# Six MLP batches begin with a product whose PSUM bank ScalarE first copies two columns of the last output into

## The chip, the core and the metric

The kernel runs on one core of one Trainium2 chip. The metric is the device time of one launch in microseconds (us); three runs of the kernel before took 1219.04, 1220.44 and 1220.67 us, median **1220.44 us**. The core's engines work beside each other and wait for each other by semaphores: TensorE multiplies (PE in the profile; the loads of its weights are listed apart, as PEld), ScalarE (ACT) casts, copies and evaluates functions, VectorE (DVE) adds and subtracts, GpSimd (POOL) does little here, and SyncE (SP) issues the transfers from the chip's memory. TensorE writes its products into eight banks of a memory called PSUM, from which ScalarE and VectorE read.

## The reference

Two residual layers with a mixer and an MLP each; the change is in the MLP, which is the last line of the loop:

```python
def reference(x, c, ada_w, ada_b, norm_mix, norm_mlp, ..., mlp_w1, mlp_w2):
    for layer in range(DEPTH):
        mod = c_act @ ada_w[layer] + ada_b[layer]
        shift1, scale1, gate1, shift2, scale2, gate2 = jnp.split(mod[:, None, :], 6, axis=-1)
        ...
        h = rms_norm(x, norm_mlp[layer]) * (1.0 + scale2) + shift2
        x = x + gate2 * (jnp.square(jax.nn.relu(h @ mlp_w1[layer])) @ mlp_w2[layer])
    return x
```

x is 512 tokens by 1024, the hidden layer has 4096 columns, and all is in 32-bit floating point.

## The kernel before

**Precision.** Every operand of a product is split in two, hi (the number rounded to the type in which TensorE multiplies) and lo (what is left). `mm3` makes one product out of three matmuls: weights hi by data hi (L290), weights hi by data lo (L291), weights lo by data hi (L292). These three lines carry nearly all that TensorE does. A weight block comes by a transfer (`raw_w`, L269, the profile's `wraw`), is cast on ScalarE to `whi` (L280) and subtracted on VectorE to `wlo` (L281); `split_w` does both, in rings of four buffers each, and `at` says at which column of its buffer the block begins: `AT512` at 0, `AT256` at 16.

**The MLP** (`mlp`, called once for each layer: about 298 to 600 us and 913 to 1220 us) goes in four batches of 1024 hidden columns. In a batch

- first come four *pairs* (`pair`; in the first batch of a layer fewer, since part of its hidden columns is made before). A pair makes 256 hidden columns of all 512 tokens by a scheme of seven products of half size. A product is 4 x 3 matmuls of 128x256. Its operands are parts of the weights (`wa`, `wb`, `wc`, `wd`) and of the data (`hT`, and sums `t1` to `t4`, the profile's `t0h` to `t3l`), where `wb` and `wc` are split from sums and differences of two weight blocks that VectorE forms in buffers called `tt` (L1081 to L1087), and `wd` (`wdh`, `wdl`) is half of a block. The banks are `a`, `b`, `c`, 256 columns each. `a` gets the first, the third, the sixth and the seventh product, and the content of `a` after the first and after the third is copied out by ScalarE (`kept`, L1114), after the first one so that the third can go on adding in the bank;
- the seventh product of a pair (`wd` by `t4`) is put off (`last`, `before()`, `rest()`) until after the second product of the next pair, or, behind the last pair of a batch, until after the first output's seventh step;
- then come the outputs: 8 (7 or 5 in a layer's last batch) sums of 128x512, each 8 x 3 matmuls with 512 columns, over the hidden columns just made. `products` runs them, `done` adds them to x on VectorE (`x_add`, L515) and asks for the weights and the bank of the output after the next (`second`).

`acc` gives out the eight banks in turn.

**What sets the order.** On TensorE the order is written out by hand: matmuls run in the order of the code. On ScalarE, VectorE and SyncE a scheduler places the instructions, which then run in that order on each engine. `tc.issue_after(i)` makes instructions begun within it stand behind `i`.

**The start of a batch.** Behind the first batch of a layer each batch is prepared while the outputs of the one before run: ahead of the products of output n-2 `pair_w` (a generator with three steps) is started and taken two steps, to `wa` and `wb`; behind that output's addition it is taken the third, to `wc` and `wd`. After the products of output n-1, and `done`, the next batch's first pair starts. There are six such starts: batches 1, 2 and 3 of both layers.

Of the kernel before, what the change touches and what calls it, by code (L numbers as in the profile page):

```python
# [220 lines left out]
def trunk(tc, x_d, c_d, rep_d, small_d, const_d, ada_d, ws_d, win_d, wv_d, woab_d, w1_d, w2_d, wqk_d, wvc_d, woc_d, out_d):  # L221
    nc = tc.nc
    act, dve, pool_e, pe, sync = nc.scalar, nc.vector, nc.gpsimd, nc.tensor, nc.sync
# [137 lines left out]
    def acc():  # L361
        return mps.tile([P, T], F32, name="acc", tag="acc", bufs=4)
# [374 lines left out]
    for j in range(2):  # L737
        copied = act.copy(Q2[:, j], sacc[6 + j])
# [250 lines left out]
    w = [load_w(woab_d[o]) for o in (0, 1, 2)]  # L989
# [78 lines left out]
    def pair_w(l, i, hp):  # L1068


        r0, r1 = raw_w(w1_d[l, 2 * i]), raw_w(w1_d[l, 2 * i + 1])
        a, b = slice(0, T), slice(T, 2 * T)

        def place():
            nsum[0] += 1
            n = (nsum[0] - 1) % 4
            return tt[:, 1024 * n:1024 * n + 1024]
        w = [split_w(r0, None, AT256)]
        yield w
        s_ = place()  # L1080
        dve.tensor_tensor(s_[:, a], r1[:, a], r1[:, b], op=ALU.add)  # L1081
        dve.tensor_tensor(s_[:, b], s_[:, a], r0[:, a], op=ALU.subtract)
        w.append(split_w(s_, None, AT256))
        yield w
        z_ = place()
        dve.tensor_tensor(z_[:, a], r0[:, b], s_[:, b], op=ALU.subtract)
        dve.tensor_tensor(z_[:, b], r0[:, a], r1[:, a], op=ALU.subtract)  # L1087
        w.append(split_w(z_, None, AT256))
        w.append([hp.tile([P, 576], F32R, name=n, tag=n)[:, 16:528] for n in ("wdh", "wdl")])
        split(r1[:, b], *w[3])  # L1090
        yield w

    def pair(i, hp, th, hid, before, steps_):


        for w in steps_:
            pass
        wa, wb, wc, wd = w
        a, b, c = [acc(256) for _ in range(3)]
        cm = [hp.tile([P, T], F32, name="cm", tag="cm", bufs=3) for _ in range(2)]  # L1100
        out = [hid_new(hp, 2 * i + j) for j in range(2)]
        hid += out
        b11 = [(hT[k], H[0]) for k in range(4)]
        b21 = [(hT[k], H[0]) for k in range(4, 8)]
        b22 = [(hT[k], H[1]) for k in range(4, 8)]
        t1, t2, t3, t4 = [[(t_, slice(256 * k, 256 * k + 256)) for k in range(4)] for t_ in th]

        def prod(ps, w, at, bs, first):
            for k, (h, sl) in enumerate(bs):
                mm3(ps, w, slice(at + k * P, at + (k + 1) * P), h, sl, first and k == 0, k == 3, skip_group_check=True)  # L1110

        def kept(ps):
            t_ = hp.tile([P, 256], F32, name="kept", tag="kept", bufs=5)
            act.copy(t_, ps)  # L1114
            return t_

        def relu2(j, sl, ps=None):
            c_ = cm[j][:, sl]
            act.activation(c_, c_ if ps is None else ps, AF.Relu)
            act.activation(c_, c_, AF.Square)  # L1120
            split(cm[j], *out[j], sl)

        prod(a, wa, 0, b11, True)
        p1 = kept(a)
        prod(c, wb, 0, t1, True)
        p5 = kept(c)
        before()
        prod(a, wb, T, t2, False)
        u2 = kept(a)
        prod(b, wa, T, b21, True)  # L1130
        dve.tensor_tensor(cm[0][:, H[0]], b, p1, op=ALU.add)
        prod(c, wc, 0, b22, False)
        dve.tensor_tensor(cm[0][:, H[1]], c, u2, op=ALU.add)
        relu2(0, FULL)
        prod(a, wc, T, t3, False)
        dve.tensor_tensor(cm[1][:, H[1]], a, p5, op=ALU.add)
        relu2(1, H[1])

        def last():
            prod(a, wd, 0, t4, False)  # L1140
            relu2(1, H[0], a)
        return last
# [15 lines left out]
    def mlp(l, last, hp, head, th, more=()):  # L1158

        nrm = Norm(1, 0, (7,)) if not last else None  # L1160
        ahead = None
        for b in range(4):
            hid, rest = list(head) if b == 0 else [], lambda: None
            if b == 0:
                for n, j in enumerate((4, 5)):
                    whole_tile(more[n] if more else load_w(w1_d[l, j]), j, hp, hid)
            for i in range(len(hid) // 2, 4):
                rest = pair(4 * b + i, hp, th, hid, rest, ahead or pair_w(l, 4 * b + i, hp))
                ahead = None
            n = 8 if b < 3 else 7 if last else 5  # L1170
            second = lambda o: (acc(), load_w(w2_d[l, b // 2, o, b % 2], None, AT256 if o == n - 1 else AT512))

            def products(p, k0, k1):
                for k in range(k0, k1):
                    mm3(p[0], p[1], ks(k), hid[k], FULL, k == 0, k == 7)

            def done(o):
                added = x_add(o, ps_[o][0], FULL, l, GATE2)
                if b == 3:
                    if last:  # L1180
                        sync.dma_start(out_d[o], x[o])
                    else:
                        nrm.add(o, FULL)
                if o + 2 < n:
                    ps_[o + 2] = second(o + 2)
                if o < len(PIECES[b]):

                    with tc.issue_after(added.ins):
                        background(PIECES[b][o])

            ps_ = {0: second(0)}
            products(ps_[0], 0, 7)
            rest()
            ps_[1] = second(1)
            products(ps_[1], 0, 7)
            for o in range(2):
                products(ps_[o], 7, 8)
                done(o)
            for o in range(2, n):
                if o == n - 2 and b < 3:  # L1200

                    ahead = pair_w(l, 4 * b + 4, hp)
                    next(ahead)
                    next(ahead)
                products(ps_[o], 0, 8)
                done(o)
                if o == n - 2 and b < 3:
                    ahead = [next(ahead)]
        if not last:
            log_exp_tables()  # L1210
        ps, banks, ws = {}, {}, []
        for o in range(n, 8):
            for hf in range(2):
                banks[bank[0] % 8] = o, hf
                ps[o, hf] = acc(256)

            ws.append(load_w(w2_d[l, 1, o, 1], None if o == n else (hp, f"t{o - 6}h", f"t{o - 6}l"), AT256))
        return nrm, ps, banks, hid, ws
# [44 lines left out]
    hp = pool("mlp0", stack=m_s)  # L1263
# [396 lines left out]
    hid = [tuple(Handle(t=t_) for t_ in hl) for hl in hk_t]  # L1660
# [11 lines left out]
    w = [weights(wqk_d[s // 2, s % 2], None, AT256) for s in range(4)]  # L1672
# [21 lines left out]
    for s_ in "v0 q2 q3 u0 u1 v1 w0 q4 v2 q5 u2 q6 u3 q7 v3 u4 u6 w1 u5 u7".split():  # L1694
        n = int(s_[1])
# [32 lines left out]
    th = [[in_h1([P, 1088], F32R, f"t{i}{a}").new(AT512) for a in "hl"] for i in range(4)]  # L1728
# [109 lines left out]
```

## Time and profile before

| | us |
|---|---|
| median of three runs | 1220.44 |
| the execution that was profiled | 1222.3 |
| its span, first to last instruction | 1220.5 |
| TensorE busy, MLP of layer 0 (298 to 600) | 301.33 of 302 |
| VectorE busy there | 212.34 |
| ScalarE busy there | 150.88 |
| TensorE busy, MLP of layer 1 (913 to 1220) | 303.98 of 307 |
| VectorE busy there | 178.08 |
| ScalarE busy there | 140.43 |

The mean clock granted to TensorE is 0.997 of full speed over the span and 1.00 in both MLP stages. The share of time in which the transfer engines are busy is 0.44 in the first stage and 0.30 in the second.

How to read it: matmuls are pipelined, each begins while the one before is still running, so a TensorE that is busy without a gap may still run its matmuls closer together or farther apart. What a stretch of matmuls costs is the distance from the start of one to the start of the next, and that is read from a stretch without a pause as its length over its number of matmuls. A row of the timeline has start, duration, engine, line, operation, output and inputs, and in brackets the idle time of the engine ahead of it with what ended it. In the rows of one line (L1114 ...) three durations stand after the count: the shortest, the middle and the longest, in ns, and then the times of the first and the last. A row of the waits has who waited, for whom, us in all, how often, and the longest.

### The profile page before, as it was taken

What the parts mean: (1) busy time and instruction counts of PE and PEld (TensorE: products, weight loads), DVE (VectorE), ACT (ScalarE), POOL (GpSimd) and SP (SyncE); (2) the same over time, 40 slices, a digit from 0 to 9 for tenths busy, and PEclk for the clock granted to TensorE, in tenths of its full rate; (3) what the DMA queues carried; (4) which work ended last, traced back from release to release, by engine and by line L of the source; (5) the groups of instructions that cost most, each with busy time, mean ns of one, the idle gap of its engine ahead of it and who ended that gap; (6) DMA issues with size and microseconds to landing.
All of it is one profiled execution on the core that took longest, in us unless ns stands there. A gap on an engine that the chain in (4) does not pass through costs nothing.

```text
span 1220.5 us, 19156 instructions
## 1 busy us (share of the span) xinstructions
PE 1205.6 (99%) x7657; PEld 1067.4 (87%) x7657; DVE 890.1 (73%) x1433; ACT 610.6 (50%) x1101; POOL 15.3 (1%) x25
## 2 busy tenths in 40 slices
PE   8999999999999999999999999999999999999998
PEld 6788877899889899898998888888998898998997
DVE  8997878769577675866768885888796575566652
ACT  4343233438247255274547764677574282472650
POOL 0000000000000000000220000000000000000000
PEclk9999999999999999999989999999999999999999
DMA  8765453612533523624435424534114233233131
GB/s 300 259 233 164 144 202 125 204 52 69 200 101 133 193 83 121 207 87 158 153 93 184 139 86 156 173 121 136 39 56 137 68 122 120 70 122 104 62 130 52
DMA packets 46330, 163.50 MB, mean 134 GB/s; under 512 B 5264, under 2 KB 5784, under 8 KB 46240
## 3 DMA queue, kind: packets, MB, share of 16 engines
q1 hardware_dynamic: 46240, 162.27, 39.9%
q8 instruction: 60, 0.98, 0.3%
q14 instruction: 30, 0.25, 0.1%
HBM read 155.96 MB, written 2.10 MB: 130 GB/s over the span
## 4 chain that ended last, share of the span: by engine, by line
PE 84%; DVE 9%; DMA 4%; ACT 2%; issue 1%; SPq 0%; ACTq 0%; DVEq 0%
PE b L290 20%; PE b L292 20%; PE b L291 20%; PE acc L290 4%; PE acc L292 3%; PE acc L291 3%; PE b L1590 1%; PE b L1569 1%; PE b L1625 1%; DMA raw<-in_ws 1%; PE b L1626 1%; PE b L1627 1%; PE b L1497 1%; DVE eraw L429 1%; DVE wlo L281 1%
## 5 line engine op out<-in xcount | busy, mean ns | idle before, releaser
L280 ACT CAST whi<-wraw 128x1024 fp32r<-128x1024 f32 x123 | 127.1, 1047 | 199.8 <-PE b L291 86.4
L290 PE MATMUL b<-hidh,whi 128*128 128x512 f32 (+1 forms) x544 | 205.5, 378 | 0.0
L291 PE MATMUL b<-hidl,whi 128*128 128x512 f32 (+1 forms) x544 | 205.3, 377 | 0.0
L292 PE MATMUL b<-hidh,wlo 128*128 128x512 f32 (+1 forms) x544 | 205.1, 377 | 0.0
L290 PE MATMUL b<-hh,whi 128*128 128x256 f32 (+1 forms) x632 | 195.7, 310 | 0.0
L291 PE MATMUL b<-hl,whi 128*128 128x256 f32 (+1 forms) x632 | 192.6, 305 | 0.6 <-DVE hl L1453 0.5
L292 PE MATMUL b<-hh,wlo 128*128 128x256 f32 (+1 forms) x632 | 192.4, 304 | 0.0
L281 DVE TENSOR_TENSOR wlo<-wraw,whi 128x1024 fp32r<-128x1024 f32 x123 | 149.4, 1221 | 44.1 <-ACT whi L280 41.5
L515 DVE SCALAR_TENSOR_TENSOR x<-b,modc,x 128x512 f32<-128x512 f32 (+1 forms) x100 | 67.8, 683 | 87.2 <-PE b L292 87.0
L291 PEld LDWEIGHTS b<-hl,whi 128*128 128x128 f32 x632 | 121.2, 192 | 5.5 <-DVE hl L1453 0.9
L290 PEld LDWEIGHTS b<-hh,whi 128*128 128x128 f32 x632 | 119.9, 190 | 5.7 <-issue 1.4
L292 PEld LDWEIGHTS b<-hh,wlo 128*128 128x128 f32 x632 | 120.0, 190 | 5.3
L292 PEld LDWEIGHTS b<-hidh,wlo 128*128 128x128 f32 x544 | 102.2, 188 | 19.3
L291 PEld LDWEIGHTS b<-hidl,whi 128*128 128x128 f32 x544 | 102.4, 188 | 18.5
L290 PEld LDWEIGHTS b<-hidh,whi 128*128 128x128 f32 x544 | 102.1, 188 | 18.7
L281 DVE TENSOR_TENSOR wlo<-tt,whi 128x1024 fp32r<-128x1024 f32 x52 | 63.5, 1220 | 30.4 <-ACT whi L280 29.5
L280 ACT CAST whi<-tt 128x1024 fp32r<-128x1024 f32 x52 | 53.3, 1048 | 61.4 <-PE b L291 50.1
L429 DVE CUSTOM_DVE_ANT_0 wraw<-wraw,cb 128x1024 f32<-128x1024 f32 x56 | 67.9, 1219 | 13.5 <-DMA wraw<-in_ada 13.4
L300 DVE TENSOR_TENSOR hidl<-cm,hidh 128x256 fp32r<-128x256 f32 (+1 forms) x90 | 44.8, 510 | 39.2 <-ACT hidh L299 37.4
L290 PE MATMUL acc<-hh,whi 128*128 128x512 f32 x128 | 52.2, 408 | 0.0
L1391 DVE TENSOR_TENSOR wlo<-raw,whi 128x1024 fp32r<-128x1024 f32 x36 | 43.8, 1220 | 9.9 <-ACT whi L1390 9.8
L292 PE MATMUL acc<-hh,wlo 128*128 128x512 f32 x128 | 49.9, 390 | 0.0
(377 smaller groups left out, 2664.2 us busy)
## 6 DMA issues: line engine op xcount, KB each, us to landing
wraw<-in_w SPq DMA_DIRECT2D x122, 512.0 KB, 3.6
wraw<-in_ada SPq DMA_DIRECT2D x56, 512.0 KB, 3.5
raw<-in_ada SPq DMA_DIRECT2D x24, 512.0 KB, 4.2
eraw<-in_ada SPq DMA_DIRECT2D x16, 512.0 KB, 3.7
wraw<-in_win SPq DMA_DIRECT2D x16, 512.0 KB, 3.4
raw<-in_wqk SPq DMA_DIRECT2D x16, 512.0 KB, 4.5
raw<-in_ws SPq DMA_DIRECT2D x8, 512.0 KB, 6.4
wraw<-in_woab SPq DMA_DIRECT2D x8, 512.0 KB, 3.9
```

Of the source, the lines that this page charges most:

```text
L280: act.copy(hi, raw)
L281: dve.tensor_tensor(lo, raw, hi.bitcast(F32), op=ALU.subtract)
L290: pe.matmul(ps, whi, h[0][:, hs], start=start, stop=False, **kw)
L291: pe.matmul(ps, whi, h[1][:, hs], start=False, stop=False, **kw)
L292: pe.matmul(ps, wlo, h[0][:, hs], start=False, stop=stop, **kw)
L300: dve.tensor_tensor(lo[:, sl], t_[:, sl], hi[:, sl].bitcast(F32), op=ALU.subtract)
L429: dve.tensor_tensor_reduce(out=raw, in0=raw, in1=cbt[0], scale=1.0, scalar=0.0, op0=ALU.mult, op1=ALU.add, accum_out=modr[:, col:col + 1])
L515: return dve.scalar_tensor_tensor(x[o][:, sl], ps, mcol(l, v, o), x[o][:, sl], op0=ALU.mult, op1=ALU.add)
L1391: on_dve(1024, lambda: dve.tensor_tensor(lo.t, raw.t, hi.t.bitcast(F32), op=ALU.subtract), (raw, hi), (lo,), 1)
L1497: pe.matmul(col.t[:, 8 * s + 2 * b:8 * s + 2 * b + 2], sq[s].t[:, ks(b)], hs2, start=True, stop=True)
L1569: pe.transpose(tp.t[:, o_:o_ + P], be.t[:, w0:w0 + P], ident)
L1590: pe.matmul(po.t[orow, P * b - t0:P * (b + 1) - t0], v.t[:, c, hcol], be.t[:, w0:w0 + P], start=first[j], stop=(c == b), skip_group_check= ...
```

## The change

Before the addition of the last output (n-1) of a batch, `mlp` takes the next bank with `acc(256)` and has ScalarE copy two columns of the last output's bank into it. This bank is then handed to the next batch's first pair, which uses it as its `a`; so no bank is used that would not have been used, and the first product overwrites what was copied. The third step of `pair_w` no longer runs behind output n-2: it runs in `pair`, within `tc.issue_after` of the copy, so the instructions that it issues on ScalarE stand behind the copy. So do those of the second pair of the batch, since `copied` is cleared only there.

```diff
-    def pair(i, hp, th, hid, before, steps_):
-
-
-        for w in steps_:
-            pass
+    copied = [None]
+
+    def pair(i, hp, th, hid, before, steps_, first=None):
+
+
+        with ExitStack() as after:
+            if copied[0] is not None:
+
+                after.enter_context(tc.issue_after(copied[0]))
+            for w in steps_:
+                pass
         wa, wb, wc, wd = w
-        a, b, c = [acc(256) for _ in range(3)]
+        if first is None:
+            copied[0] = None
+        a, b, c = [acc(256) if n or first is None else first for n in range(3)]
...
-        ahead = None
+        ahead = bank_ = None
...
-                rest = pair(4 * b + i, hp, th, hid, rest, ahead or pair_w(l, 4 * b + i, hp))
-                ahead = None
+                rest = pair(4 * b + i, hp, th, hid, rest, ahead or pair_w(l, 4 * b + i, hp), bank_)
+                ahead = bank_ = None
...
                 products(ps_[o], 0, 8)
+                if o == n - 1 and b < 3:
+
+
+                    bank_ = acc(256)
+                    copied[0] = act.copy(bank_[:, 0:2], ps_[o][0][:, 0:2]).ins
                 done(o)
-                if o == n - 2 and b < 3:
-                    ahead = [next(ahead)]
```

The order of instructions on TensorE, SyncE and GpSimd is the same as before. It moves on ScalarE and VectorE. The line numbers below are those of each kernel's own file: what is L1114 before is L1122 after the change, and what is L1131 is L1139.

ScalarE at the start of the first of the six batches, before. `x4` means four such rows in a run; `b_3140` is the bank `a` of the batch's first product.

```order
L280 CAST whi<-wraw 128x1024 x4
L299 CAST wdh<-wraw 128x512
L280 CAST whi<-wraw 128x1024
L280 CAST whi<-tt 128x1024 x2
L280 CAST whi<-wraw 128x1024
L1114 COPY kept<-b_3140 128x256
L1114 COPY kept<-b_3142 128x256
L280 CAST whi<-tt 128x1024
L1114 COPY kept<-b_3140 128x256
```

The same place after. `b_3059` is the bank of the last output, `b_3129` the bank of the first product.

```order
L280 CAST whi<-wraw 128x1024 x5
L280 CAST whi<-tt 128x1024
L1218 COPY b_3129<-b_3059 128x2
L280 CAST whi<-tt 128x1024
L299 CAST wdh<-wraw 128x512
L280 CAST whi<-wraw 128x1024
L1122 COPY kept<-b_3129 128x256
L1122 COPY kept<-b_3143 128x256
L280 CAST whi<-tt 128x1024
L1122 COPY kept<-b_3129 128x256
```

The copy has come in, and the casts of the third weights (the second `whi<-tt`) and of `wdh` now stand behind it, together with the cast for the next pair's first weights and ahead of the first `kept`.

VectorE at the same place, before; `x_66` to `x_68` are the additions of the last three outputs to x (`b_3059` again the last output's bank), `cm<-b_...,kept` the additions of a pair.

```order
L515 SCALAR_TENSOR_TENSOR x_66<-b_2995,modc,x_66 128x512
L281 TENSOR_TENSOR wlo<-tt,whi 128x1024
L1082 TENSOR_TENSOR tt<-tt,wraw 128x512
L1086 TENSOR_TENSOR tt<-wraw,tt 128x512
L1081 TENSOR_TENSOR tt<-wraw 128x512
L1082 TENSOR_TENSOR tt<-tt,wraw 128x512
L515 SCALAR_TENSOR_TENSOR x_67<-b_3027,modc,x_67 128x512
L281 TENSOR_TENSOR wlo<-tt,whi 128x1024
L1086 TENSOR_TENSOR tt<-wraw,tt 128x512
L1087 TENSOR_TENSOR tt<-wraw 128x512
L515 SCALAR_TENSOR_TENSOR x_68<-b_3059,modc,x_68 128x512
L281 TENSOR_TENSOR wlo<-wraw,whi 128x1024
```

The same place after.

```order
L515 SCALAR_TENSOR_TENSOR x_66<-b_2995,modc,x_66 128x512
L281 TENSOR_TENSOR wlo<-tt,whi 128x1024
L1086 TENSOR_TENSOR tt<-wraw,tt 128x512
L515 SCALAR_TENSOR_TENSOR x_67<-b_3027,modc,x_67 128x512
L515 SCALAR_TENSOR_TENSOR x_68<-b_3059,modc,x_68 128x512
L281 TENSOR_TENSOR wlo<-tt,whi 128x1024
L300 TENSOR_TENSOR wdl<-wraw,wdh 128x512
L281 TENSOR_TENSOR wlo<-wraw,whi 128x1024
L281 TENSOR_TENSOR wlo<-tt,whi 128x1024
L1139 TENSOR_TENSOR cm<-b_3142,kept 128x256
L281 TENSOR_TENSOR wlo<-tt,whi 128x1024
L1141 TENSOR_TENSOR cm<-b_3143,kept 128x256
```

The third weights' subtraction and that of `wdl` now stand behind the last addition to x, which the copy precedes; the operations on `tt` that prepare a later pair no longer stand between the last additions but later in the batch.

## The prediction, made before the changed kernel was run

> **What bounds the kernel now.** I read the page first: engine shares, granted clock, chain.
>
> ```profile
> PE 1205.6 (99%) x7657; PEld 1067.4 (87%) x7657; DVE 890.1 (73%) x1433; ACT 610.6 (50%) x1101; POOL 15.3 (1%) x25
> PEclk9999999999999999999989999999999999999999
> PE 84%; DVE 9%; DMA 4%; ACT 2%; issue 1%; SPq 0%; ACTq 0%; DVEq 0%
> ```
>
> TensorE is busy nearly always, at the full clock, and carries 84% of the chain. ScalarE has half its time free. The change touches only the two MLP stages, so next I asked who TensorE waits for there (298 to 600 us, then 913 to 1220 us); each answer has one row.
>
> ```profile
> PE b L292 <- DVE wlo L281: 0.7, 1, 0.7
> PE b L292 <- DVE wlo L281: 0.3, 1, 0.3
> ```
>
> One microsecond in 609. Both waits stand in a first batch; at the six batch starts that the change edits, TensorE waits for nothing. So no wait is there to remove, and a gain can only come from matmuls that follow each other faster. Busy time does not show that, since matmuls are pipelined, so I divided stretches without a pause by the matmuls that start in them. The table by windows has stretch, length, busy time (count), clock, DMA share and GB/s; its count includes one to three matmuls still running from before.
>
> ```profile
> 352.93:391.09 38.16, 38.16 (x325) 1.00 0.30 99
> 1133.61:1171.77 38.16, 38.16 (x326) 1.00 0.30 99
> 282.26:287.70 5.44, 5.44 (x50) 1.00 0.01 3
> 302.35:307.79 5.44, 5.44 (x51) 1.00 0.39 133
> 916.41:921.85 5.44, 5.44 (x51) 1.00 0.36 112
> 312.57:313.98 1.41, 1.41 (x13) 1.00 0.00 0
> 604.88:607.83 2.95, 2.95 (x27) 1.00 0.00 0
> ```
>
> The first two rows are the pair products of the first and the last of the six batches: 27 products of 12 matmuls, 128x256 each (the 28th runs later, between two outputs). 38.16 us over 324 matmuls is 117.8 ns each. The next three rows hold 48 matmuls of the same shape, same offset of weights to operand and same clock: 5.44/48 = 113.3 ns. **So TensorE has two spacings for this product, 4% apart, and each holds as long as nothing interrupts.** What precedes the short ones is seen in the timeline.
>
> ```profile
> 299.81 1.23 DVE L281 TENSOR_TENSOR wlo<-tt,whi 128x1024 fp32r<-128x1024 f32 x1 [0.39 <-ACT whi L280]
> 300.02 0.28 PE L290 MATMUL b<-t0h,whi 128*128 128x256 f32 x1
> 300.14 0.28 PE L291 MATMUL b<-t0l,whi 128*128 128x256 f32 x1
> 301.09 0.19 PEld L292 LDWEIGHTS b<-t0h,wlo 128*128 128x128 f32 x1 [0.87 <-DVE wlo L281]
> 301.09 0.38 PE L292 MATMUL b<-t0h,wlo 128*128 128x256 f32 x1 [0.67 <-DVE wlo L281]
> 301.31 0.28 PE L290 MATMUL b<-t0h,whi 128*128 128x256 f32 x1
> 301.43 0.29 PE L291 MATMUL b<-t0l,whi 128*128 128x256 f32 x1
> 301.67 0.28 PE L290 MATMUL b<-t0h,whi 128*128 128x256 f32 x1
> 301.78 0.28 PE L291 MATMUL b<-t0l,whi 128*128 128x256 f32 x1
> ...
> 915.15 0.39 PE L292 MATMUL b<-t0h,wlo 128*128 128x256 f32 x1 [0.31 <-DVE wlo L281]
> ...
> 280.60 0.28 PE L290 MATMUL b<-hh,whi 128*128 128x256 f32 x1
> 280.89 0.38 PE L291 MATMUL b<-hl,whi 128*128 128x256 f32 x1
> ```
>
> A weight load waits for its wlo (the DVE operation ends at 301.04, the load starts 0.05 later); the next matmul comes 0.22 later instead of 0.118; after a few more the spacing is 0.11, and 113.3 ns until 307.79. Before the pause it was 0.12. The stretches at 916 and 282 us follow restarts too: 915.15 waited for a wlo, and 280.89 came 0.29 after its predecessor. The last row of the window table does not fit:
>
> ```profile
> 604.36 0.28 PE L290 MATMUL b<-hh,whi 128*128 128x256 f32 x1
> 604.65 0.39 PE L291 MATMUL b<-hl,whi 128*128 128x256 f32 x1
> 604.88 0.29 PE L292 MATMUL b<-hh,wlo 128*128 128x256 f32 x1
> ```
>
> This too restarts after a wait (0.29 instead of 0.118, then 0.23), and goes on at 2.95/25 = 118.0 ns. So a restart can change the spacing and need not. Three of these four ended short.
>
> **The change part by part.** (a) *The pause.* The first matmul of a batch now waits for ScalarE's copy, which waits for the last matmul of the last output.
>
> ```profile
> 352.70 0.39 PE L292 MATMUL b<-hidh,wlo 128*128 128x512 f32 x1
> 352.93 0.28 PE L290 MATMUL b<-hh,whi 128*128 128x256 f32 x1
> 353.13 0.75 DVE L515 SCALAR_TENSOR_TENSOR x<-b,modc,x 128x512 f32<-128x512 f32 x1 [0.91 <-PE b L292]
> L1114 ACT COPY kept<-b x78: 347/367/374, 301.6 to 1167.9; 128x256 f32<-128x256 f32 x78
> L1595 ACT CAST oT<-b x24: 249/266/382, 665.0 to 864.9; 128x128 fp32r<-128x128 f32 x16, 128x256 fp32r<-128x256 f32 x8
> L595 ACT ACTIVATE lbe<-lbe x1: 213/213/213, 60.4 to 60.4; 128x12 f32<-128x12 f32 x1
> ```
>
> The matmul of 352.70 is the last of the output; the addition to x, which waits for it, starts 0.43 later. The copy starts then, since in before ScalarE is free there: 0.43. No row shows a copy of two columns: 128x256 from a bank takes 0.367, 128x128 0.266, which puts 2 columns at 0.17 by their line; the smallest row is 0.213, the next 0.25. I take 0.20, nearest the smallest, and keep 0.17 to 0.27. Then 0.05 to the load, as at 301.04. The first matmul starts 0.43+0.20+0.05 = 0.68 after the last instead of 0.23, and the second 0.22 after it instead of 0.118: 0.45+0.10 = **0.55 us a batch, 3.3 in six** (3.1 to 3.7).
>
> The Trainium skill, page "ScalarE: Activation LUTs", section "Rules for kernel authors", budgets about 0.3 us for each ACTIVATE plus 0.83 ns an element; if that held for the copy, the pause would be about 0.65, an estimate, and the six 0.6 us dearer. The 0.213 row lies below it.
>
> (b) *The spacing.* Where a restart ends short, 324 matmuls go from 117.8 to 113.3: 38.16 - 36.72 = 1.44 us, less about 0.02 until it settles. Net a batch: 1.42 - 0.55 = **0.87 gained, or 0.55 lost** where it stays long. The row of 312.57 is a 28th product, behind the short stretch and an output's 128x512 matmuls: 1.41/12 = 117.5 ns, long again. So the 128x512 matmuls end the short state, every batch begins anew, and the 28th product gains nothing.
>
> The Trainium skill, page "TensorE: Matmul & The Clock Gate", section "Step-by-step: what each phase is for", says that TensorE has two independent read ports, so that loading the next weights takes no bandwidth from the running matmul. By that rule the spacing would depend on shape and clock alone, and the pause would be pure loss, the second rival below. The 117.8 and 113.3 ns at one clock speak against it.
>
> (c) *Weights behind the copy.* The casts of wdh and of the third weights (whi from tt), with their two DVE subtractions, move from ahead of the batch to behind the copy, and the cast of the next pair's whi stands behind them; ahead of kept, whose reader is the third product.
>
> ```profile
> 352.95 1.05 ACT L280 CAST whi<-wraw 128x1024 fp32r<-128x1024 f32 x1 [4.54 <-PE b L291]
> 354.55 0.37 ACT L1114 COPY kept<-b 128x256 f32<-128x256 f32 x1 [0.55 <-PE b L292]
> 365.74 0.62 ACT L299 CAST wdh<-wraw 128x512 fp32r<-128x512 f32 x1 [0.22 <-PE b L291]
> 367.70 2.00 ACT L280 CAST whi<-tt 128x1024 fp32r<-128x1024 f32 x2
> ```
>
> Two casts of 1.05 take 2.00, so the next starts about 0.1 before one ends. With L for the start of the batch's first load, the third weights' cast starts at L-0.15, wdh at +0.80, the next whi at +1.32, kept at +2.27 and ends at +2.64; with 0.05 the third product may load at +2.69. It wants to at 0.22+22x0.1133 = +2.72 with the short spacing, +2.82 with the long. **That is free, by 0.03 us only**, where in before kept, done at 354.92, had 0.7 to spare. If it is late, the third product restarts too: 0.1 to 0.2 a batch, and the spacing is decided again. The third weights' wlo is there by L+2.2 (cast ends +0.90, DVE 1.22), wanted by the fifth product at +5.5; wdl is wanted after eight products. Neither shows.
>
> (d) *DVE.* Its last addition to x waits for the copy, which reads the same bank: 0.2 later, and behind it stands the third wlo, which waits for its cast anyhow. Four tt operations of a later pair move into the batch:
>
> ```profile
> 347.69 0.69 DVE L1081 TENSOR_TENSOR tt<-wraw 128x512 f32<-128x512 f32 x1 [0.34 <-DMA wraw<-in_w]
> ```
>
> Four times 0.69 is 2.8 us of VectorE; the casts that read them stood at 367.70, 15 us behind the start. Free. SP's DMA order and POOL are unchanged.
>
> **The sum.** With k of six batches short: 3.3 - 1.42 k. Six: -5.2; five: -3.8; four: -2.4; three: -1.0; two: +0.5; none: +3.3. The profiled execution took 1222.3 us with a span of 1220.5, the three runs' median is 1220.44; I carry the difference to the median. Three of four restarts short is a rate under which five of six or four come out, and the 604 case paused only 0.17 us, with its predecessor still in the pipe, while 301 and 915 waited longer, as these will. So five: 1220.4 - 3.8 = **1216.6 us**.
>
> **Rivals.** *A coin.* If the state depends on where in some finer rhythm the load restarts (the second matmul comes 0.22 behind the restart at 301.09, 0.23 at 604.65), half the batches flip: two to four, 1218.0 to 1220.9. For it: 604. Against: the three others.
> *Pure loss, slower than before.* The restarts seen stood at the second or third matmul of a triple inside a product; these stand at a product's first, behind a 128x512 run. If the state follows from what ran before, or from the weights' place, all stay long: 1220.4+3.3 = 1223.7. It decides as soon as at most one batch flips (1222.3). For it: all six batches and the first product of each first batch run long directly behind 128x512. Against: 301 and 915 had come from that too, and flipped at the pause.
> *The copy delays nothing*, if TensorE's first matmul does not wait for it: 1220.4. Against: it writes into that product's bank.
> *kept late:* +0.6 to +1.2 in all, 1217.2 to 1217.8 on the forecast; inside the range.
>
> **Numbers.** Five or six short 0.50; two to four 0.28; one or none 0.20; no pause 0.02. Six would be 1215.2, with a copy of 0.17 1215.0. The range takes in the cases down to one flip: 1214.8 to 1222.4. It leaves out no flip at all and a little below 1214.8, some 2 in 10. A measurement of this kernel tells 0.2%, 2.4 us, from no change, so four flips (1218.0) stand on the line: faster 0.56, same 0.27, slower 0.17.
>
> **What would show it.** (a) at each of six batch starts a wait of TensorE for the copy, 0.68 from matmul to matmul; a copy much over 0.27 or a start later than 0.43 refutes the price. (b) windows over the 27 products of 36.7 us against 38.16, batch by batch; all at 38.2 would be the second rival. (c) a wait of the third product for kept, if my 0.03 was wrong. (d) any wait for wlo or wdl behind the start would refute that they are free. The forecast is wrong if fewer than four batches run at 113.3.

## The result and the profile after

The changed kernel took 1224.32 us (median of six runs, 1221.73 to 1226.59) beside 1220.53 for the kernel before: a ratio of **1.0037** with a 95% interval of 1.0023 to 1.0051, so it is slower, by 2.8 to 6.2 us. That is outside the range on record, and near the rival "pure loss" (1223.7). Run unaltered again, on three chips, it took 1215.5 us on one, 1217.0 and 1218.0 on the second, and 1224.2 on the third; the last section of the experiments tells what the traces show of that.

The profiled execution took 1226.6 us with a span of 1224.9. Of its page, the engine shares, the granted clock and the chain:

```profile
PE 1207.1 (99%) x7657; PEld 1067.2 (87%) x7657; DVE 887.1 (72%) x1433; ACT 609.3 (50%) x1107; POOL 15.3 (1%) x25
PEclk9999999999999999999989999999999999999999
PE 85%; DVE 8%; DMA 4%; ACT 2%; issue 1%; SPq 0%; ACTq 0%; DVEq 0%
```

Nothing in them has moved by more than a point. The waits of TensorE in the first MLP stage (who waited, for whom, us in all, times, longest) show one new row, the first below, which the second stage repeats; the second row stood there before:

```profile
PE b L290 <- ACT b L1218: 0.7, 3, 0.2
PE b L292 <- DVE wlo L281: 0.4, 1, 0.4
```

Three waits of 0.2 us in each stage. They are smaller than what they cost, since a matmul is counted as busy until it leaves the pipeline. The timeline at the start of the first of the six batches has the true distances:

```profile
353.97 0.39 PE L292 MATMUL b<-hidh,wlo 128*128 128x512 f32 x1
354.40 0.14 ACT L1218 COPY b<-b 128x2 f32<-128x2 f32 x1 [10.17 <-PE b L292]
354.57 0.75 DVE L515 SCALAR_TENSOR_TENSOR x<-b,modc,x 128x512 f32<-128x512 f32 x1 [4.84 <-ACT b L1218]
354.59 0.38 PE L290 MATMUL b<-hh,whi 128*128 128x256 f32 x1 [0.23 <-ACT b L1218]
354.81 0.28 PE L291 MATMUL b<-hl,whi 128*128 128x256 f32 x1
354.93 0.28 PE L292 MATMUL b<-hh,wlo 128*128 128x256 f32 x1
...
356.88 0.36 ACT L1122 COPY kept<-b 128x256 f32<-128x256 f32 x1
...
357.52 0.28 PE L290 MATMUL b<-t1h,whi 128*128 128x256 f32 x1
```

From the last matmul to the first it is 0.62 us, then 0.22, then 0.12 again: the pause is there, and the spacing behind it is the old one. `kept` ends at 357.24, and the third product begins at 357.52 without a wait. The windows over the 27 products of the first and the last of the six batches, and over one whole batch from start to start (length, busy time and count, weight loads, DVE, ACT, POOL, clock, DMA share, GB/s):

```profile
354.59:392.86 38.27, 38.27 (x325) 38.27 (x325) 30.94 (x46) 30.34 (x57) 0.00 (x0) 1.00 0.34 113
1137.79:1176.05 38.26, 38.26 (x324) 38.26 (x325) 30.93 (x46) 30.33 (x57) 0.00 (x0) 1.00 0.34 112
354.59:438.40 83.81, 83.57 (x528) 75.56 (x529) 58.53 (x87) 41.22 (x74) 0.00 (x0) 1.00 0.42 139
```

All six batches take 38.26 or 38.27: the old 38.16 and 0.10 of the restart's second distance. The same batch from start to start in the kernel before:

```profile
352.93:436.24 83.31, 83.31 (x529) 75.64 (x528) 58.72 (x86) 41.37 (x72) 0.00 (x0) 1.00 0.41 139
```

A batch took 83.31 before and takes 83.81 now, **0.50 us more, 3.0 in six**. The rest of the 4.3 us between the two profiled executions stands ahead of the first of the six starts: the last matmul before it begins at 352.70 in the kernel before and at 353.97 here, 1.27 later, and 0.9 of that was there by 60 us, ahead of any edit (a matmul that starts at 58.72 before starts at 59.59 after).

In what follows a batch is called short when its 27 products take 36.8 us (113.3 ns a matmul) and long at 38.2 (117.8).

### The profile page after: what moved, and what is told of

Read it like the earlier page. It is cut to its first block, busy times and chain, and to the rows that moved or that the text cites. A ratio compares the mean times of both kernels' runs of the same rounds, so it can differ in the third digit from the quotient of the medians.

```text
span 1224.9 us, 19159 instructions
## 1 busy us (share of the span) xinstructions
PE 1207.1 (99%) x7657; PEld 1067.2 (87%) x7657; DVE 887.1 (72%) x1433; ACT 609.3 (50%) x1107; POOL 15.3 (1%) x25
## 4 chain that ended last, share of the span: by engine, by line
PE 85%; DVE 8%; DMA 4%; ACT 2%; issue 1%; SPq 0%; ACTq 0%; DVEq 0%
PE b L290 20%; PE b L291 20%; PE b L292 20%; PE acc L290 4%; PE acc L291 4%; PE acc L292 4%; PE b L1601 1%; PE b L1580 1%; PE b L1636 1%; PE b L1637 1%; PE b L1638 1%; PE b L1508 1%; DVE eraw L429 1%; DMA raw<-in_ws 1%; PE lv L821 1%; PE b L1552 1%
```

## Experiments

Where a distance is given in whole ns, it is the difference of the start times of two TensorE records in the trace, which have 1 ns; the rows print 0.01 us. "The gap" is the distance from the last matmul of a batch's last output to the first matmul of the next batch. Runs e1 to e4 were on one chip, called A here, e5 to e8 on B, e9 to e11 and e15 to e17 on C, e12 to e14 on D, e18 on E; of the first measurement the chip is not known. The `+` and `-` lines are against the changed kernel, and `...` stands for lines that are not shown.

### e1, e5: the weights behind the copy without the wait

In e1 the copy goes to a small new tile, and the first pair takes its bank as before. A flag `fresh` keeps the weights of both pairs behind the copy, as in the changed kernel:

```diff
-    copied = [None]
+    copied, fresh = [None], [False]
...
-        if first is None:
+        if not fresh[0]:
             copied[0] = None
+        fresh[0] = False
...
-                    bank_ = acc(256)
-                    copied[0] = act.copy(bank_[:, 0:2], ps_[o][0][:, 0:2]).ins
+                    fresh[0] = True
+                    two = hp.tile([P, 2], F32, name="two", tag="two")
+                    copied[0] = act.copy(two, ps_[o][0][:, 0:2]).ins
```

> The copy goes to a small tile that nobody reads, and the first pair takes its bank as before; ScalarE's and VectorE's order is that of the changed kernel, but TensorE no longer waits for the copy. Theory 'the pause is all': the weights behind the copy are free, no wait at the six starts (last matmul to first 0.23), the time is that of the kernel before, 1220.5, ratio 1.000 within 0.15%. Rival 'the moved weights cost too': a part of the 3.8 us stays, ratio 1.001 or more, and a wait for kept, wlo or wdl stands behind the starts.

The median was 1224.06 against 1221.55, ratio 1.0015 (1.0004 to 1.0027), as the rival had it; but no wait stood behind the starts. The windows over one output of 24 matmuls, of e1, of the kernel before, and over a batch of e1:

```profile
403.80:409.30 5.50, 5.50 (x25) 4.51 (x24) 5.18 (x11) 0.00 (x0) 0.00 (x0) 1.00 0.38 125
```

```profile
402.76:408.20 5.44, 5.44 (x25) 4.51 (x24) 5.16 (x11) 0.00 (x0) 0.00 (x0) 1.00 0.42 123
```

```profile
353.86:437.59 83.73, 83.73 (x530) 75.64 (x528) 58.44 (x86) 41.18 (x73) 0.00 (x0) 1.00 0.42 139
```

The outputs had become slower, 229 ns a matmul against 227, and that makes the 0.42 us of a batch. The new tile was at fault: in e1's program 264 of the 1440 wide matmuls (128x512) of the MLPs read hidden tiles whose place had moved by an odd multiple of 32 bytes (not the 8 bytes of e5's expectation below). In most outputs concerned these are six in a row: the first six, the seventh to twelfth or the thirteenth to eighteenth. In the trace the slow matmuls of such an output, 228 to 236 ns, begin just there (a batch's first and last output apart, which have other slow ones in the kernel before too). e5 copies the two columns onto themselves, so that no tile is added; the flag is that of e1:

```diff
-                    bank_ = acc(256)
-                    copied[0] = act.copy(bank_[:, 0:2], ps_[o][0][:, 0:2]).ins
+                    fresh[0] = True
+                    copied[0] = act.copy(ps_[o][0][:, 0:2], ps_[o][0][:, 0:2]).ins
```

> The run with the small tile was no clean test: with the tile allocated, the 128x512 products of the outputs took 5.51 us each instead of 5.44, although no wait was added, since what lies behind the tile moved by 8 bytes. Here the two columns are copied onto themselves in the last output's bank, no tile is added, and the first pair takes its bank as before. Theory 'the pause is all': outputs back at 5.44 us, no wait at the six starts, batch to batch 83.31 us as before, ratio 1.000 within 0.15%. Rival 'the moved weights cost': batch to batch above 83.31, or a wait behind the starts, ratio 1.001 or more.

1220.54 against 1221.32, ratio 0.999 (0.9978 to 1.0001). A batch of e5:

```profile
354.34:437.64 83.30, 83.30 (x529) 75.63 (x528) 58.53 (x86) 41.21 (x73) 0.00 (x0) 1.00 0.42 139
```

It takes 83.30 us, as before, and TensorE has no new wait. One order on ScalarE differs from the changed kernel's: the cast for the next pair's weights stands behind the first `kept` and not ahead of it, but in the changed kernel nobody waits for that `kept` either. **The moved weights and the moved operations of VectorE are free**; what the change costs or brings is in the wait for the copy.

### e2: the copy and the wait alone

The third weights and wdh are split behind output n-2 as in the kernel before; the copy stays.

```diff
-            if copied[0] is not None:
-
-                after.enter_context(tc.issue_after(copied[0]))
+            pass
...
                 done(o)
+                if o == n - 2 and b < 3:
+                    ahead = [next(ahead)]
```

> The copy and the wait as in the changed kernel, but the third weights and wdh are split where the kernel before does it. On ScalarE the cast of the next pair's weights (1.05 us) then stands directly ahead of the copy and begins 0.02 after the first matmul did. Theory 'ScalarE's order': the copy starts about 1 us later, the pause from matmul to matmul is about 1.6 instead of 0.625, and the time is 1224.3 + 6 x 1.0 = 1230. Rival 'the move does nothing': 0.625 as in the changed kernel. For the spacing the pause is another length: theory 'phase' has no forecast batch by batch but expects some of six at 36.7 us; theory 'place' has all six at 38.1 to 38.2.

From the timeline of e2 at the first start:

```profile
354.90 0.39 PE L292 MATMUL b<-hidh,wlo 128*128 128x512 f32 x1
355.14 1.04 ACT L280 CAST whi<-wraw 128x1024 fp32r<-128x1024 f32 x1 [4.54 <-PE b L291]
356.10 0.16 ACT L1216 COPY b<-b 128x2 f32<-128x2 f32 x1
356.30 0.39 PE L290 MATMUL b<-hh,whi 128*128 128x256 f32 x1 [1.01 <-ACT b L1216]
```

The cast for the next pair's weights slips in front of the copy, as expected, and the gap is 1.40 us (1.36 in layer 1) instead of 0.625. That is what the moved weights are for: behind the copy they keep this cast away from it. But the one run took 1222.5 us, not 1230, because **all six batches were short**, at 36.84. So a restart at a product's first matmul, behind 128x512, can end short: the theory "place" fell here, with the same two columns.

### e3, e4, e7, e8: the number of columns

```diff
-                    copied[0] = act.copy(bank_[:, 0:2], ps_[o][0][:, 0:2]).ins
+                    width = (3, 4, 5, 6, 7, 8)[3 * l + b]
+                    copied[0] = act.copy(bank_[:, 0:width], ps_[o][0][:, 0:width]).ins
```

> As the changed kernel, but the copy has 3, 4, 5, 6, 7, 8 columns in the six batches, which moves the restart by about 0.9 ns a column (145 ns for 2, 367 for 256). Theory 'phase' (the spacing is decided by when, in a rhythm of some 5 to 10 ns, TensorE restarts; a fixed chain of copy and wait hits one phase each time): some of the six batches run their 27 products in 36.7 us, and the outcome goes with the number of columns. Theory 'place' (a restart at the first matmul of a product behind 128x512 always ends long): all six 38.1 to 38.2 us. Theory 'chance' (each restart by itself, half and half): about three of six, without an order; but then six of six long in the changed kernel was a chance of 1 in 64.

> The same with 9, 10, 12, 16, 64 and 256 columns; the last two lengthen the pause by about 0.05 and 0.22 us. Theory 'phase': some batches at 36.7 us. Theory 'place': none. Theory 'length' (a pause must be long enough for TensorE's pipeline to run empty; 301 and 915 waited 0.6 to 0.95 from matmul to matmul against 0.625 here): the batch of 256 columns, and it alone or with 64, at 36.7.

With 3 to 8 columns the six batches were long, short, short, short, long, short; with 9, 10, 12, 16, 64 and 256 all were short. Single runs took 1217.3 and 1221.4 us; that e4's took longer, with more short batches, does not come from the batches: its first one begins at 356.50 us and that of e3 at 352.36, so 4 us lie ahead of it, and between the starts of the third and the fourth e4 takes 2.5 us more, with the third short in both. A column costs 0.83 ns: of e4's copies (shortest, middle, longest in ns) the last has 256 columns,

```profile
L1219 ACT COPY b<-b x6: 151/156/357, 356.3 to 1133.6; 128x9 f32<-128x9 f32 x1, 128x10 f32<-128x10 f32 x1, 128x12 f32<-128x12 f32 x1, 128x16 f32<-128x16 f32 x1
```

against 145 for 2 in the changed kernel: 212 ns for 254 columns. Is it the width or the batch that counts? e7 moves the same six widths by three batches, e8 tries the guess that every fourth width is long:

> Widths 6, 7, 8, 3, 4, 5 in the six batches: those of 3 to 8 moved by three batches. Theory 'phase by width': short, long, short, long, short, short (long where the copy has 7 and 3 columns). Theory 'batch': long, short, short, short, long, short as before. Theory 'chance': no agreement with either.

> Widths 11, 15, 19, 10, 14, 18. Long so far: 2, 3, 7 columns; short: 4, 5, 6, 8, 9, 10, 12, 16, 64, 256. Theory 'rhythm of four columns' (3.3 ns, 8 TensorE cycles): 11, 15 and 19 long, 10, 14, 18 short. Theory 'only near a threshold': a copy of more than 7 columns always ends short, all six short. Theory 'chance': no order.

The windows of e7 (6, 7, 8, 3, 4, 5 columns), then of e8 (11, 15, 19, 10, 14, 18):

```profile
354.61:391.46 36.85, 36.85 (x325) 36.85 (x325) 30.55 (x46) 30.08 (x57) 0.00 (x0) 1.00 0.35 116
437.00:475.26 38.26, 38.26 (x324) 38.26 (x325) 30.94 (x46) 30.34 (x57) 0.00 (x0) 1.00 0.36 113
520.81:557.65 36.84, 36.84 (x325) 36.84 (x325) 30.55 (x46) 30.09 (x57) 0.00 (x0) 1.00 0.35 116
964.06:1002.33 38.27, 38.27 (x325) 38.27 (x325) 30.95 (x46) 30.36 (x57) 0.00 (x0) 1.00 0.34 113
1047.87:1084.71 36.84, 36.84 (x324) 36.84 (x325) 30.65 (x46) 30.09 (x57) 0.00 (x0) 1.00 0.36 117
1130.26:1167.10 36.84, 36.84 (x325) 36.84 (x325) 30.55 (x46) 30.09 (x57) 0.00 (x0) 1.00 0.34 116
```

```profile
354.67:392.93 38.26, 38.26 (x324) 38.26 (x325) 30.95 (x46) 30.35 (x57) 0.00 (x0) 1.00 0.34 113
438.48:476.75 38.27, 38.27 (x325) 38.27 (x325) 30.97 (x46) 30.36 (x57) 0.00 (x0) 1.00 0.34 113
522.30:560.56 38.26, 38.26 (x324) 38.26 (x325) 30.95 (x46) 30.35 (x57) 0.00 (x0) 1.00 0.33 113
967.70:1004.52 36.82, 36.82 (x324) 36.82 (x325) 30.53 (x46) 30.08 (x57) 0.00 (x0) 1.00 0.35 116
1050.07:1086.92 36.85, 36.85 (x324) 36.85 (x325) 30.63 (x46) 30.08 (x57) 0.00 (x0) 1.00 0.36 117
1132.48:1169.30 36.82, 36.82 (x324) 36.82 (x325) 30.54 (x46) 30.08 (x57) 0.00 (x0) 1.00 0.35 116
```

Twelve batches, twelve as "phase by width" and "rhythm of four columns" said; "batch", "threshold" and "chance" fall. The long gaps of e7 and e8 are 625, 628, 632, 635 and 639 ns: **every 3.3 ns, four columns' time of the copy, comes an instant at which a restart ends long; between two of them it ends short.** By that one in four of the instants that copies of different width can hit is a bad one. A single gap is too coarse to tell them apart, since it is good to 1 ns: 12 columns in e4 show 632 too and were short.

### e6: four columns in all six batches

```diff
-                    copied[0] = act.copy(bank_[:, 0:2], ps_[o][0][:, 0:2]).ins
+                    copied[0] = act.copy(bank_[:, 0:4], ps_[o][0][:, 0:4]).ins
```

> The changed kernel with a copy of 4 columns instead of 2 in all six batches. Theory 'phase': the width decides, and 4 was short in its one batch, so all six batches take 36.84 us for their 27 products; gap 626 ns against 231, so 0.395 lost and 1.32 gained a batch, 0.925 net, 5.5 us in six: 1216.0 against 1221.5, ratio 0.9955 within 0.0015. Theory 'chance': about three or four of six short, ratio 0.998 to 1.0. Theory 'batch' (the place of a batch decides, not the width): the first batch of layer 0 and the second of layer 1 stay long, as with 3 to 8 columns; four short, 0.998.

1215.41 against 1221.32, ratio **0.9952** (0.9938 to 0.9965). The 27 products of the first batch, and that batch from start to start:

```profile
352.53:389.38 36.85, 36.85 (x325) 36.85 (x325) 30.55 (x46) 30.09 (x57) 0.00 (x0) 1.00 0.35 116
```

```profile
352.53:434.92 82.39, 82.15 (x529) 74.13 (x529) 58.20 (x87) 41.17 (x74) 0.00 (x0) 1.00 0.42 141
```

All six are short, with the same pause at the same place: 83.31 - 82.39 = 0.92 us gained a batch, 5.5 in six, as expected. In its trace gaps of 626 ns stand against 625 of the changed kernel's.

### e9, e10, e11: far widths, two copies, the last output's weights elsewhere

e9 is the edit of e3 with widths of 1, 2, 255, 127, 128 and 25.

> Widths 1, 2, 255, 127, 128, 25. Theory 'rhythm of four columns' (3 more than a multiple of 4 ends long, however long the copy): 255 and 127 long beside 128 short, 25 short; 2 long in its second batch as in all six of the changed kernel; 1 is open (if 1, 2 and 3 columns take the same least time, long). Rival 'long pauses end short' (64 and 256 columns did): 255, 127, 128 all short.

255 was long, with a gap of 835 ns, and 128, 25 and 1 were short, so it is not a matter of length. From 3 columns to 255 are 63 times four, and the gap grows by 835 - 625 = 210 ns, 3.33 ns for each four. Two were missed: 127, and 2, which was short here.

e10 puts a second copy ahead, of 4 to 9 columns, and leaves 3 columns in the one that TensorE waits for:

```diff
-                    copied[0] = act.copy(bank_[:, 0:2], ps_[o][0][:, 0:2]).ins
+                    width = (4, 5, 6, 7, 8, 9)[3 * l + b]
+                    act.copy(ps_[o][0][:, 0:width], ps_[o][0][:, 0:width])
+                    copied[0] = act.copy(bank_[:, 0:3], ps_[o][0][:, 0:3]).ins
```

> The copy into the first product's bank has 3 columns in all six batches, but ahead of it on ScalarE stands a copy of 4, 5, 6, 7, 8, 9 columns of the last output's bank onto themselves, which moves the restart and not the size of the last write. Theory 'time' (the instant of the restart in the rhythm decides): not all long; batches with 4 and 8 columns alike, those with 5 and 9 alike, one class of the four long. Rival 'bytes' (a copy of 3 columns more than a multiple of four leaves something that TensorE pays for): all six long.

Five were short and the last, with 9 columns ahead, long. So the size of the written piece does not decide, and "bytes" falls. That 5 and 9 were to be alike was wrong: a rhythm by width would make one of 4 to 7 long. The gaps are 804, 804, 806, 806, 807 and 809 ns; by steps of 3.33 from 625 the bad instants would stand near 805 and 808 (an estimate), so the jump from 804 to 806 goes past the first of them. That fits "time", though records of 1 ns do not prove it.

e11 has 4 to 9 columns and puts the last output's weights at column 0:

```diff
-            second = lambda o: (acc(), load_w(w2_d[l, b // 2, o, b % 2], None, AT256 if o == n - 1 else AT512))
+            second = lambda o: (acc(), load_w(w2_d[l, b // 2, o, b % 2], None, AT512 if o < n - 1 or b < 3 else AT256))
```

> The weights of the last output of six batches stand at column 0 of their buffer like those of the other outputs, instead of 16; the copy has 4, 5, 6, 7, 8, 9 columns. The last output takes 24 x 226.7 instead of 24 x 233.3 ns, 0.16 us less a batch. Theory 'rhythm of TensorE's own matmuls' (the restart counts from the last matmul's place): the same rule as before, 7 columns long, the others short, as the chain from the last matmul is the same. Rival 'the class moves': another one of the four classes is long, since the last matmul stands elsewhere in the rhythm.

7 columns were long and the others short, as without this edit: which width is long does not change when the last output's matmuls take 226.7 ns instead of 233.3. But its gaps are 1 or 2 ns smaller at the same width (624 for 4 columns instead of 626, 627 for 7 instead of 628), and 625 was short here, with 5 columns. So gaps can be compared only between kernels that are alike in the last output. The run took 1214.6 us.

### e12 to e18: the same kernel again

The misses with 2 and 127 columns asked whether the first measurement stands. e12, e15, e16 and e18 are the changed kernel, unaltered; e13 is e6 again; e14 has 4 columns and the last output's weights at column 0; e17 is the edit of e3 with 2, 3, 127, 7, 11 and 10 columns.

> The changed kernel once more, its copy of 2 columns as it is. Six of six batches were long in its trace, but 2 columns ended short in their one batch with 1, 2, 255, 127, 128, 25, and 127 did too, which the rhythm of four columns forecast long. Theory 'the class belongs to the kernel': all six long again, 1224 or 1.003 against before in every round. Theory 'one tick of margin' (the same chain can restart one column's time earlier or later from launch to launch): batches of both kinds in the trace, or times of two kinds, 1216 and 1224, between which the median falls.

> The copy of 4 columns once more. Theory 'the class belongs to the kernel': all six short, 0.995 against before. Theory 'one tick of margin': if the chain can come one tick early, 4 columns act as 3 and end long in some batches, and the ratio is nearer to 1.

> The copy of 4 columns, and the last output's weights at column 0 of their buffer, which made its 24 matmuls 0.13 us shorter with the other widths. All six batches short as with 4 columns there, 6 x 0.13 = 0.8 us below the kernel with 4 columns: 1214.6 against 1221.4, ratio 0.9945 within 0.0015. If the class moves with the last output's place: some or all six long, 1.002.

e12 gave 1215.52 against 1221.50, ratio **0.9952** (0.9935 to 0.9970), all six runs at 1217.5 or below: the changed kernel, slower on the first chip, is faster here. Its first and last batch:

```profile
354.08:390.90 36.82, 36.82 (x324) 36.82 (x325) 30.54 (x46) 30.08 (x57) 0.00 (x0) 1.00 0.35 116
1127.58:1164.40 36.82, 36.82 (x324) 36.82 (x325) 30.62 (x46) 30.08 (x57) 0.00 (x0) 1.00 0.34 116
```

e13 gave 0.9948 (0.9931 to 0.9965), six short. e14 gave **1213.63 us, 0.9938** (0.9921 to 0.9955), six short; its batch,

```profile
352.12:434.35 82.23, 81.99 (x528) 74.13 (x529) 58.29 (x87) 41.09 (x74) 0.00 (x0) 1.00 0.42 141
```

is 0.16 us below that of e6 (its gaps are 624 ns, as e11's with 4 columns). Then chip C again, with the changed kernel loaded twice, and another one:

> The changed kernel unaltered, on whatever chip comes. Times near 1224 (six batches at 38.27) or near 1215.5 (six at 36.83). Theory 'the chip decides' (the wait crosses from one engine's clock to the other's, and on some chips the crossing costs one column's time more): all launches here are of one kind, the same as in the next run. Theory 'each loading decides': this and the next run may differ.

> The same kernel loaded once more on the same chip. 'The chip decides': the same kind as the run before it. 'Each loading decides': the other kind about as often as not, over this, the run before it and their timed launches.

> Widths 2, 3, 127, 7, 11, 10 on the same chip. Rhythm of four columns: 3, 7, 11 long and 10 short on every chip; 2 and 127 stand at the edge: 2 of the same kind as in the two runs before it if the chip decides; 127 long where 2 is long and short where 2 is short (they were short together in e9), if one shift moves them both.

> The changed kernel unaltered, once more, on whatever chip comes. Theory 'the chip decides': if it is a chip on which it was short, short again in all six batches and in all timed launches, about 1216 to 1218; on another chip all six of one kind, short or long, and the timed launches of that kind too. Theory 'each launch decides': six of one kind in the trace, but timed launches of both kinds, some 8 us apart beyond the spread that the kernel before shows.

On chip C all twelve batches of e15 and e16 started short, and eleven stayed so; the third of e16 waited 0.2 us for a `kept` of its last pair and went on long, 37.48 in all (ratios 0.9972, 0.9947 to 0.9997, and 0.9965, 0.9942 to 0.9988). On chip E all six were long, eight runs from 1221.4 to 1226.3, ratio 1.0028 (1.0013 to 1.0043); the first of them:

```profile
355.36:393.63 38.27, 38.27 (x325) 38.27 (x326) 30.96 (x46) 30.34 (x57) 0.00 (x0) 1.00 0.33 113
```

Apart from that batch of e16, in no loading did the six batches differ. The gaps of the five loadings of the one program, in ns (a single one can be off by the rounding of 1 ns, so the means count):

```
first measurement  625 625 624 625 625 625   mean 624.8   six long    1224.3 us
e18  chip E        625 625 625 625 625 625   mean 625.0   six long    1224.2
e12  chip D        624 625 624 624 624 624   mean 624.2   six short   1215.5
e15  chip C        625 624 624 624 625 624   mean 624.3   six short   1218.0
e16  chip C        624 624 624 624 625 624   mean 624.2   six short   1217.0
3 columns (e3 A, e7 B, e17 C)   625 625 625               all long
```

Where the changed kernel is long, its first matmul comes about 0.7 ns later, nearly the time of one column, and stands where 3 columns stand on the other chips. e17 shows the same blur: 2 and 127 were short together and 3 and 11 long, as expected, but 7 short and 10 long, both missed; 10 had a gap of 632, which is 11's, and 7 one of 629 where it had been long at 628. So the instant fits where the width alone does not, and the width decides only up to about one column's time. 127 columns, long by the rhythm of four and short at gaps of 729 (e9) and 728, are not explained; by steps of 3.33 from 625 a bad instant would stand at 728.3 (an estimate), which such gaps can't tell from its neighbours.

Where the time is lost can be read from the same records, with the copy's own start and end. In the first measurement the copy starts 427.7 ns (mean of six) behind the last matmul, in e18 and the three short loadings 426.3 to 426.8. In e18 the first matmul comes 53.5 ns behind the copy's end, in the other four loadings 52.2 to 52.5. And in the two missed batches of e17 the copy starts at 428 ns, in its other four at 426 or 427. So, as far as records of 1 ns tell, the late step is the copy's start in the first measurement and in e17, and TensorE's restart in e18.

That the chip decides which it is fits two loadings on C and the timed runs on D and E. But e17 lost a column's time in two batches of six on chip C, within one launch; what sets it, and whether one chip ever gives the unaltered kernel both ways, stays open.

## Why the prediction was wrong

- **What bounds.** Right: no wait was removed, and the whole question was the spacing.
- **(a) The pause.** Right in its steps, 10% too long. The copy starts 0.43 behind the last matmul as said, but takes 0.145 us instead of 0.20, below both ends of its range; from matmul to matmul it is 0.62 against 0.68, and the next distance is 0.22 as said. So a batch costs 0.50, not 0.55. The Trainium skill's 0.3 us for each ACTIVATE ("ScalarE: Activation LUTs", "Rules for kernel authors") is twice what this copy took, which the profile lists as a COPY.
- **(b) The spacing.** The size was right wherever it came: 36.83 where 36.72 + 0.02 + 0.10 was forecast, and with 4 columns 0.92 net a batch against 0.87. The Trainium skill's two independent read ports ("TensorE: Matmul & The Clock Gate", "Step-by-step: what each phase is for"), as the prediction drew on them, would have made every pause pure loss; e6's 36.85 against 38.16 at one clock disagrees with that. What makes the two spacings, and the rhythm that chooses between them, no run shows.
- **(c), (d) The weights and VectorE.** Right: `kept` ended 2.65 us behind the first load (forecast 2.64), no one waited, and e5 shows the move free.
- **The sum is the step that failed**: "Three of four restarts short is a rate under which five of six or four come out". The rate was about right; that the six are six draws was wrong. The restarts it was read from wait for weights whose time varies from launch to launch: over all 20 traces those near 302 and 915 us were long 14 times in 40 (9 and 5), and in e15 and e16, one program on one chip, the one near 915 was long in the first and short in the second. The one at 301 us, short in the trace of before, was long in that of after (its row stands below). The copy's restart hangs on nothing but the last matmul, by a chain that is the same to about 1 ns, so all six batches hit one instant and end alike: six of six in all five loadings, but for the later wait in e16. The forecast had to be all or none, with about one chance in four for none, 1223.7, and a range that held it. No row of the trace of before says which of the two would come.
- **The rivals.** "A coin" named the cause, a finer rhythm, but drew six times too. "Pure loss" had the number by luck and not the cause: e2 and e6 are short at the very place where it said that all stay long. "The copy delays nothing" did not occur; "kept late" did once in 19 traces, in e16, and in a batch's last pair, not at its start.

The 48 matmuls behind the restart near 302 us in the changed kernel, which took 5.44 us in the kernel before:

```profile
302.35:308.00 5.65, 5.65 (x50) 5.65 (x50) 4.83 (x6) 4.81 (x8) 0.00 (x0) 1.00 0.41 125
```

Of the slowdown, 3.0 us are shown to be the pauses (batch by batch); the interval of 2.8 to 6.2 holds that, and what is above it was not traced to the edit.

## What to carry to other kernels

When a trace shows the same work at two speeds, ask what each start hangs on before counting how often each came: here starts that hung on weights arriving were draws, and starts that hung on a fixed chain were one draw, repeated. A pause that is meant to set a state should be aimed at the middle of the instants that work, not at one that works on the chip at hand: here 2 columns stand one column's time from a bad instant, and the same program gained 0.5% on one chip and lost 0.3% on another. 4 columns were short in all twelve batches of e6 and e13, on two chips; neither they nor e14 were tried on a chip where 2 are long, and 5, a column farther from 3, ran in a few batches only.

## What the runs showed that was not expected

- A rhythm of about 3.3 ns in TensorE's restarts: two starts less than 1 ns apart make 324 matmuls run at 117.8 or at 113.3 ns, until matmuls of another shape follow.
- The identical program on different chips, 1224 and 1215.5 to 1218 us, with the kernel before at 1220.5 to 1222.4 on all of them.
- A tile of two columns that nobody reads cost 0.42 us a batch, and the matmuls that slowed down begin with those whose operand moved by an odd multiple of 32 bytes (e1). A copy added for a test is better made in place.
- A ScalarE copy from one bank to another takes 0.145 us for 2 columns and 0.83 ns for each further one.
